# Layer 0's modulation by single row tiles, five summed on TensorE and three as dot products on VectorE, and the first projection in the order of arrival

## The chip, the core and the metric

The kernel runs on one core of a Trainium2 chip. The core has five engines that run at the same time, each through its own list of instructions in a fixed order: TensorE (PE in the profile, with its weight loads as PEld), VectorE (DVE), ScalarE (ACT), GpSimd (POOL) and SyncE (SP), which issues all of this kernel's DMAs. Engines wait for each other through semaphores. The metric is the device time of one execution in microseconds (us); before the change it is 1154.92 us, the median of 3 runs (1154.86 to 1157.67).

## What is computed

Two layers of a transformer-like trunk over 512 latent and 256 context tokens of 1024 channels. Each layer starts with a modulated norm and one combined input projection; two attention branches, gates and an output projection follow. The change touches only what stands ahead of and inside the first projection of layer 0:

```
mod_x = silu(c) @ w_ada + b_ada            # w_ada: 1024 x 3072
shift_x, scale_x, gate_x = split(mod_x, 3)
mod_c = silu(c_ctx) @ w_ada + b_ada
hx = rmsnorm(x, norm_g) * (1 + scale_x) + shift_x
hc = rmsnorm(ctx, norm_g) * (1 + scale_c) + shift_c
px = hx @ w_in ;  pc = hc @ w_in           # first 512 columns: a_k
```

The modulation is a vector times a matrix, for two vectors (c and c_ctx). Its shift and scale parts for layer 0 need 1024 x 2048 numbers of w_ada, 8 MB.

## The kernel before

The 1024 channels are cut into eight slices k of 128, and the 768 tokens into six tiles t of 128. A normed token tile is turned (transposed on PE, L287) into `yT`, where the channels lie on the partitions; so one slice of `hx` needs shift and scale of its 128 channels alone. Every operand of a projection is split into a high and a low part in fp32r, and each product is three matmuls (high by high, high by low, low by high; L341 to L343, the helper `mm3`). The first projection (columns C_AK, 512 of them) keeps six PSUM tiles open, one for each token tile, and adds to each of them slice by slice: 8 slices x 6 tiles x 3 = 144 matmuls.

Its weights come slice by slice (`load_w`): a DMA of 256 KB into one of three `raw` tiles (L309), a cast to `whi` on ACT (L311), and the rest `wlo = raw - whi` on POOL or DVE in turn (L314). A `raw` tile is free for the next load only when its `wlo` is done.

The modulation of layer 0 goes in four parts q of two slices each (`ada_load`, `ada_part`). A part's 2 MB of w_ada come as two DMAs of 1 MB (`rawx`, `rawy`). PE multiplies them by silu(c) and silu(c_ctx), which stand as columns in `scol`, on four column groups of its array side by side (L190); ACT copies the result to a row (L192), PE turns the row (L195), DVE adds the four groups (L197), and `mod_finish` (L171 to L173) makes `modc`, shift and scale. `start_mod` then scales a slice of `yT` on DVE (L298), casts it to the high part of `hx` on ACT (L300) and subtracts for the low part on DVE or POOL (L301). `start_y` (L281 to L289) squares a token tile on ACT, takes the root on POOL, scales on DVE and turns on PE.

The order of the instructions on each engine is set when the program is built, by a scheduler that plays the kernel through with its own costs and times. On the chip each engine keeps to that order: an instruction whose inputs are late holds up all that stand behind it on its engine.

## Time and profile before

| | |
|---|---|
| median of 3 runs | 1154.92 us |
| the profiled execution: its span, first to last instruction | 1153.4 us |
| PE busy | 1123.0 us (97%) |
| DVE busy | 809.8 us (70%) |
| ACT, POOL busy | 573.9 us (50%), 495.0 us (43%) |
| DMA | 134.04 MB, mean 116 GB/s |
| matmuls of the first projection start | 20.70 us |
| first matmul of the next projection (into the next psf tile) | 65.99 us |

Times of the trace are us from the start of the span. A row of the timeline is: start, duration, engine, line, operation, output <- inputs, shapes, how many in a row, and in brackets the idle time before it and what ended it. A duration includes a tail that overlaps the engine's next instruction: matmuls of 0.39 us follow each other every 0.23 us, and VectorE's of 0.69 us every 0.61 us. Rows that are cut out of the list of groups give count, busy time and mean ns of one.

### The profile page before, as it was taken

The page shows a single profiled execution, that of the slowest core. Times are in us where ns is not written, and L with a number is a line of the kernel's source. Part 1 is how long each engine was busy: PE and PEld are TensorE (multiplying, and loading weights), DVE is VectorE, ACT ScalarE, POOL GpSimd, SP SyncE. Part 2 cuts the span into 40 slices and gives each one's busy share as a digit, 9 for nine tenths or more (in the row PEclk, how much of TensorE's full clock was granted, in tenths as well). Part 3 has the DMA queues.
Part 4 walks back from the last instruction along what each step waited for, and adds up shares of the span by engine and source line. Part 5 has one row for each costly group of instructions (what it writes and reads, how often), then busy time and mean ns, then how long its engine had stood idle before and what let it go on. Part 6 is the DMA issues. An engine that isn't in the chain of part 4 may idle for free.

```text
span 1153.4 us, 17280 instructions
## 1 busy us (share of the span) xinstructions
PE 1123.0 (97%) x6078; PEld 949.0 (82%) x6078; DVE 809.8 (70%) x1508; ACT 573.9 (50%) x1167; POOL 495.0 (43%) x459
## 2 busy tenths in 40 slices
PE   5999999999999999999999999999999999999998
PEld 4688888889988888878788787888888988887786
DVE  4566688897464687688587755469787665898563
ACT  5453266666433465566330265346666445766521
POOL 3362354454375243354411126245553664465311
PEclk9999999999999999999999999999999999999999
DMA  9644222233342332470353523543332333142143
GB/s 368 195 126 137 69 85 65 72 115 97 115 130 63 107 102 73 67 276 19 121 172 101 174 74 110 176 106 113 108 105 84 110 101 101 65 173 92 63 129 92
DMA packets 88000, 134.04 MB, mean 116 GB/s; under 512 B 10629, under 2 KB 52585, under 8 KB 86249
## 3 DMA queue, kind: packets, MB, share of 16 engines
q1 hardware_dynamic: 87912, 132.94, 36.8%
q8 instruction: 48, 0.79, 0.3%
q14 instruction: 40, 0.32, 0.1%
HBM read 115.58 MB, written 17.32 MB: 115 GB/s over the span
## 4 chain that ended last, share of the span: by engine, by line
PE 83%; DVE 7%; issue 3%; POOL 2%; ACT 2%; DMA 2%; ACTq 0%; POOLq 0%; DVEq 0%
PE psx L341 12%; PE psx L343 12%; PE psx L342 12%; PE psf L341 9%; PE psf L342 9%; PE psf L343 9%; PE pst L655 5%; PE pss L704 2%; PE pss L705 2%; PE psv L959 2%; PE psv L958 1%; PE pss L781 1%; PE pst L417 1%; DVE wlo L328 1%; DVE ptl L659 1%
## 5 line engine op out<-in xcount | busy, mean ns | idle before, releaser
L659 DVE TENSOR_TENSOR ptl<-pst,pth 128x512 fp32r<-128x512 f32 (+1 forms) x176 | 116.0, 672 | 46.4 <-ACT pth L658 45.4
L658 ACT CAST pth<-pst 128x512 fp32r<-128x512 f32 (+1 forms) x176 | 99.2, 576 | 87.5 <-PE pst L655 56.3
L328 POOL TENSOR_TENSOR wlo<-raw,whi 128x512 fp32r<-128x512 f32 x68 | 95.0, 1402 | 108.9 <-ACT whi L326 87.8
L341 PE MATMUL psf<-hx,whi 128*128 128x512 f32 (+1 forms) x368 | 139.2, 378 | 0.0
L342 PE MATMUL psf<-hx,whi 128*128 128x512 f32 (+1 forms) x368 | 138.1, 375 | 0.0
L343 PE MATMUL psf<-hx,wlo 128*128 128x512 f32 (+1 forms) x368 | 137.8, 374 | 0.0
L341 PE MATMUL psx<-whi,hx 128*128 128x512 f32 (+1 forms) x368 | 137.2, 374 | 0.0
L342 PE MATMUL psx<-wlo,hx 128*128 128x512 f32 (+1 forms) x368 | 135.8, 369 | 0.0
L343 PE MATMUL psx<-whi,hx 128*128 128x512 f32 (+1 forms) x368 | 133.6, 369 | 0.0
L314 POOL TENSOR_TENSOR wlo<-raw,whi 128x512 fp32r<-128x512 f32 x44 | 60.4, 1373 | 140.4 <-ACT whi L311 123.8
L311 ACT CAST whi<-raw 128x512 fp32r<-128x512 f32 x96 | 58.7, 623 | 103.5 <-PE psx L343 38.6
L326 ACT CAST whi<-raw 128x512 fp32r<-128x512 f32 x136 | 82.5, 622 | 50.3 <-DMA raw<-in_w_in_dram 34.1
L655 PE MATMUL pst<-ident,p 128*128 128x128 f32 x640 | 99.9, 272 | 1.4 <-DVE ptl L659 0.9
L328 DVE TENSOR_TENSOR wlo<-raw,whi 128x512 fp32r<-128x512 f32 x68 | 70.2, 1033 | 28.3 <-ACT whi L326 27.8
L655 PEld LDWEIGHTS pst<-ident,p 128*128 128x128 f32 x640 | 77.7, 141 | 13.3 <-DVE ptl L659 1.6
L644 POOL TENSOR_SCALAR r<-r 128x1 f32<-128x1 f32 x64 | 23.1, 361 | 151.7 <-DVE r L639 144.1
L645 POOL TENSOR_TENSOR p<-p,r 128x512 f32<-128x512 f32 (+1 forms) x64 | 83.5, 1304 | 5.0
L341 PEld LDWEIGHTS psx<-whi,hx 128*128 128x128 f32 x368 | 69.6, 189 | 11.8 <-issue 0.8
L343 PEld LDWEIGHTS psf<-hx,wlo 128*128 128x128 f32 x368 | 69.4, 188 | 11.8
L343 PEld LDWEIGHTS psx<-whi,hx 128*128 128x128 f32 x368 | 69.4, 189 | 11.5
L342 PEld LDWEIGHTS psx<-wlo,hx 128*128 128x128 f32 x368 | 69.6, 189 | 11.0
L341 PEld LDWEIGHTS psf<-hx,whi 128*128 128x128 f32 x368 | 69.4, 189 | 10.8 <-ACT zt L502 0.2
(239 smaller groups left out, 3033.4 us busy)
## 6 DMA issues: line engine op xcount, KB each, us to landing
raw<-in_w_in_dram SPq DMA_DIRECT2D x168, 256.0 KB, 2.9
rawb<-in_w_ada_dram SPq DMA_DIRECT2D x64, 256.0 KB, 2.8
gs<-zt SPq DMA_DIRECT2D x32, 256.0 KB, 2.0
raw<-in_w_out_dram SPq DMA_DIRECT2D x32, 256.0 KB, 2.8
tg<-gs SPq DMA_DIRECT2D x4, 1536.0 KB, 7.4
rawx<-in_w_ada_dram SPq DMA_DIRECT2D x4, 1024.0 KB, 7.2
rawy<-in_w_ada_dram SPq DMA_DIRECT2D x4, 1024.0 KB, 12.2
raw<-in_w_o_a_dram SPq DMA_DIRECT2D x16, 256.0 KB, 2.7
```

The lines of the kernel that those rows point to most:

```text
L311: S.copy(hi[:, :n], raw[:, :n])
L314: e.tensor_tensor(lo[:, :n], raw[:, :n], F(hi[:, :n]), ALU.subtract)
L326: S.copy(hi, raw)
L328: lo_eng(i).tensor_tensor(lo, raw, F(hi), ALU.subtract)
L341: T.matmul(ps, lhs[0], rhs[0], start=first, stop=False)
L342: T.matmul(ps, lhs[0], rhs[1], start=False, stop=False)
L343: T.matmul(ps, lhs[1], rhs[0], start=False, stop=last)
L644: G.tensor_scalar(r[:, i:i + 1], r[:, i:i + 1], 0.5, None, ALU.mult)
L645: G.tensor_tensor(p[:, c0:c1], p[:, c0:c1], r[:, i:i + 1].to_broadcast([128, c1 - c0]), ALU.mult)
L655: T.transpose(pt[:, c0:c0 + 128], src, ident)
L658: S.copy(hi[:, n0:n1], pt[:, n0:n1])
L659: V.tensor_tensor(lo[:, n0:n1], pt[:, n0:n1], F(hi[:, n0:n1]), ALU.subtract)
```

## The change

The eight slices of the modulation now go one by one.

- Slices 0 to 4 (`ADA_PE = 5`) go as before over PE, but by single slices: a slice has its own 1 MB of w_ada in two DMAs, 8 matmuls of 256 columns (`ada_sum_pe`), and two transposes, a reduction and `mod_finish` (`ada_turn`). The program's input `w_ada0` is laid out for that and holds five slices.
- Slices 5 to 7 (`ada_wide`, `ada_dots`) take another way: w_ada comes turned, with the channel to be summed along the row, as two tiles of 128x1024 for each slice (one for shift, one for scale), and DVE multiplies each with silu(c) and with silu(c_ctx), spread over all partitions in `cb`, and sums along the row: four dot products of 1024 elements per slice, 12 in all. `cb` is 1 MB, read by two more DMAs.
- The loads, the transposes, the sums and the matmuls of the first projection are written out in one list (`start_run`), and `in_program_order` binds PE and SP to this list. DVE, ACT and POOL are still ordered by the scheduler.
- One more buffer for token tiles (`XB` 6 to 7), which the wide tiles share.

The rest of the program keeps its instructions, and nearly all of its order.

```
--- before.py
+++ after.py
@@ -30,8 +30,9 @@
 GQ_POOL = (1, 3)
 GATES = (3, 3)
 PRE_NA, PRE_GQ = 1, 2
-ON_PE, ON_DVE = mybir.EngineType.PE, mybir.EngineType.DVE
-XB, RX = 6, 2
+ON_PE, ON_DVE, ON_SP = mybir.EngineType.PE, mybir.EngineType.DVE, mybir.EngineType.SP
+XB, RX = 7, 2
+ADA_PE = 5
 
 C_AK, C_AV, C_BKV, C_AQ, C_BQ, C_AZ, C_BZ, C_GA, C_GB = (
     0, 512, 1024, 1280, 1792, 2304, 2816, 3328, 4352)
...
@@ -141,7 +140,6 @@
     csl = stp.tile([16, 128], F32, name="csl")
     V.scalar_tensor_tensor(csl, cth, 1.0, crow, ALU.add, ALU.mult)
     V.tensor_scalar(csl, csl, 0.5, None, ALU.mult)
-    nc.sync.dma_start(cd, csl)
     asum = cp.tile([128, 24, 2, 2], F32, name="asum")
     scol = stp.tile([128, 8, 32], F32, name="scol")
     V.memset(scol, 0.0)
...
@@ -172,31 +170,55 @@
         V.tensor_tensor(sc, sums[:, 1].rearrange("p k v -> p v k"), row(bsc[:, l, k0:k1]), ALU.add)
         V.tensor_tensor(sc, sc, row(g32[:, l, k0:k1]), ALU.mult)
 
-    def ada_load(q, pool):
+    ada_w, ada_pt = {}, {}
+
+    def ada_load(k, pool):
+
+        w = (pool.tile([128, 2048], F32, tag="rawx", name=nm("rawx"), bufs=RX) if k < RX
+             else big("rawy")[:, 0:2048]).rearrange("p (k n) -> p k n", k=8)
+        for h in range(2):
+            nc.sync.dma_start(w[:, 4 * h:4 * h + 4], w_ada0[k, :, 4 * h:4 * h + 4, :])
+        ada_w[k] = w
+
+    def ada_sum_pe(k, pool):
+
+        pt = psw(256, "t")
+        w = ada_w.pop(k)
+        for h in range(2):
+            for j in range(4):
+                T.matmul(pt[32 * j:32 * j + 32], scol[:, 4 * h + j, :], w[:, 4 * h + j, :], start=h == 0, stop=h == 1)
+        row = pool.tile([128, 256], F32, tag="row", name=nm("row"), bufs=1)
+        S.copy(row, pt)
+        ada_pt[k] = row
+
+    def ada_turn(k, pool):
+
+        row = ada_pt.pop(k)
+        pt = psw(256, "t")
+        for f in range(2):
+            T.transpose(pt[:, 128 * f:128 * f + 128], row[:, 128 * f:128 * f + 128], ident)
+        sums = pool.tile([128, 2, 1, 2], F32, tag="sums", name=nm("sums"))
+        V.tensor_reduce(sums.rearrange("p a k v -> p (a k) v"),
+                        pt.rearrange("p (f j v) -> p f v j", f=2, j=4)[:, :, 0:2, :], AX, ALU.add)
+        mod_finish(0, sums, k, k + 1)
+
+    def ada_wide(k, pool):
 
         ws = []
-        for h in range(2):
-            w = (pool.tile([128, 2048], F32, tag="rawx", name=nm("rawx"), bufs=RX) if h == 0
-                 else big("rawy")[:, 0:2048]).rearrange("p (k n) -> p k n", k=4)
-            nc.sync.dma_start(w, w_ada0[q, :, 4 * h:4 * h + 4, :])
+        for a in range(2):
+            w = pool.tile([128, DM], F32, tag="x", name=nm("wx"), bufs=XB)
+            nc.sync.dma_start(w.rearrange("p (h n) -> p h n", h=2), w_ada[0, :, 8 * a + k].rearrange("h p n -> p h n"))
             ws.append(w)
-        return ws
-
-    def ada_part(q, ws, pool):
-
-        pt = psw(512, "t")
-        for h, w in enumerate(ws):
-            for j in range(4):
-                T.matmul(pt[32 * j:32 * j + 32], scol[:, 4 * h + j, :], w[:, j, :], start=h == 0, stop=h == 1)
-        row = pool.tile([128, 512], F32, tag="row", name=nm("row"), bufs=1)
-        S.copy(row, pt)
-        pt = psw(512, "t")
-        for f in range(4):
-            T.transpose(pt[:, 128 * f:128 * f + 128], row[:, 128 * f:128 * f + 128], ident)
-        sums = pool.tile([128, 2, 2, 2], F32, tag="sums", name=nm("sums"))
-        V.tensor_reduce(sums.rearrange("p a f v -> p (a f) v"),
-                        pt.rearrange("p (f j v) -> p f v j", f=4, j=4)[:, :, 0:2, :], AX, ALU.add)
-        mod_finish(0, sums, 2 * q, 2 * q + 2)
+        ada_w[k] = ws
+
+    def ada_dots(k, cb, pool):
+
+        sums = pool.tile([128, 2, 1, 2], F32, tag="sums", name=nm("sums"))
+        for a, w in enumerate(ada_w.pop(k)):
+            for v in range(2):
+                o = w if v else pool.tile([128, DM], BF16, tag="jk", name=nm("jk"), bufs=1)
+                V.tensor_tensor_reduce(o, w, cb[:, v, :], 1.0, 0.0, ALU.mult, ALU.add, sums[:, a, 0, v:v + 1])
+        mod_finish(0, sums, k, k + 1)
 
     def ada_steps(l, tiles, halves, nv, pool):
 
...
@@ -384,6 +400,16 @@
                 tc.add_manual_dep(i, last, mybir.DependencyInfo(
                     mybir.DependencyClass.NoSync, mybir.DependencyReason.DATA), reason="program order")
                 last = i.name
+
+    def in_program_order(engines, n):
+
+        last = {}
+        for i in nc.cur_bb.bb.instructions[n:]:
+            if i.engine in engines:
+                if i.engine in last:
+                    tc.add_manual_dep(i, last[i.engine], mybir.DependencyInfo(
+                        mybir.DependencyClass.NoSync, mybir.DependencyReason.DATA), reason="program order")
+                last[i.engine] = i.name
 
     def turn_late(n):
 
...
@@ -581,14 +607,8 @@
         kav = big("ka").rearrange("p (j n) -> p j n", j=4)
         if first:
             w, pss = [], [psw() for t in range(6)]
-            for q in range(4):
-                if q == 0:
-                    mid(0, lambda: w.extend(load_w(W, C_AK, 512, 2, mix_lo)))
-                if q < 3:
-                    mid(q + 1, lambda: w.extend(load_w(W, C_AK, 512, 2, mix_lo, 2 * q + 2)))
-                start_mods(q)
-                for t in range(6):
-                    tok_mm(pss[t], w, 512, a_hx, t, 2 * q, 2 * q + 2)
+            mid(lambda k: w.extend(load_w(W, C_AK, 512, 1, mix_lo, k)),
+                lambda t, k: tok_mm(pss[t], w, 512, a_hx, t, k, k + 1))
             es_n.close()
             st_es.close()
             hp["p"] = bgp_es.enter_context(tc.tile_pool(name=f"cp{l}", bufs=1, reuse_waits="tile"))
...
@@ -1039,26 +1059,99 @@
                 run(late, len(late))
 
 
-    ada_w = {}
-
-    def start_part(q, load):
-
-        if q == 0:
-            ada_w[0] = ada_load(0, npool)
-            load()
-            for t in range(2, 6):
-                load_x(t)
-            ada_w[1] = ada_load(1, npool)
-            for t in range(2):
-                start_y(t, npool, yT)
-        else:
-            load()
-            if q < 3:
-                ada_w[q + 1] = ada_load(q + 1, npool)
-        ada_part(q, ada_w.pop(q), npool)
-        if q == 0:
-            for t in range(2, 6):
-                start_y(t, npool, yT)
+    def start_run(load_k, mm):
+
+        on_pe = lambda fn, *a: fn(*a)
+        n0 = len(nc.cur_bb.bb.instructions)
+
+        def ys(*ts):
+            for t in ts:
+                on_pe(start_y, t, npool, yT)
+
+        def mods(k, *cuts):
+            start_mod(k, yT, hx0, *cuts)
+
+        def mms(ts, ks):
+            for k in ks:
+                for t in ts:
+                    on_pe(mm, t, k)
+
+        add = lambda k: on_pe(ada_sum_pe, k, npool)
+        trn = lambda k: on_pe(ada_turn, k, npool)
+        load_x(0)
+        ada_load(0, npool)
+        load_x(1)
+        load_k(0)
+        ada_load(1, npool)
+        load_k(1)
+        nc.sync.dma_start(cd, csl)
+        load_x(2)
+        load_x(3)
+        ys(0)
+        add(0)
+        trn(0)
+        mods(0, 0, 128)
+        ys(1)
+        mms((0,), (0,))
+        add(1)
+        mods(0, 128, 256)
+        ada_load(2, npool)
+        load_k(2)
+        mms((1,), (0,))
+        trn(1)
+        mods(1, 0, 256)
+        load_x(4)
+        load_x(5)
+        ys(2)
+        mms((0, 1), (1,))
+        ys(3)
+        mods(0, 256, 512)
+        mods(1, 256, 512)
+        ada_load(3, npool)
+        load_k(3)
+        cb = npool.tile([128, 2048], F32, tag="rawx", name=nm("cbw"), bufs=RX).rearrange("p (v n) -> p v n", v=2)
+        for v in range(2):
+            nc.sync.dma_start(cb[:, v, :], cd[8 * v:8 * v + 8].rearrange("k p -> (k p)").unsqueeze(0)
+                              .to_broadcast([128, DM]))
+        add(2)
+        mms((2, 3), (0,))
+        trn(2)
+        mods(2, 0, 512)
+        mms((2, 3), (1,))
+        ys(4)
+        mms((0, 1), (2,))
+        ys(5)
+        ada_load(4, npool)
+        load_k(4)
+        mms((2, 3), (2,))
+        add(3)
+        for k in range(3):
+            mods(k, 512, 768)
+        mms((4, 5), (0,))
+        trn(3)
+        mods(3, 0, 768)
+        ada_wide(5, npool)
+        load_k(5)
+        mms((4, 5), (1, 2))
+        add(4)
+        mms((0, 1, 2), (3,))
+        trn(4)
+        mods(4, 0, 768)
+        ada_wide(6, npool)
+        load_k(6)
+        mms((3, 4, 5), (3,))
+        ada_dots(5, cb, npool)
+        mods(5, 0, 768)
+        ada_wide(7, npool)
+        load_k(7)
+        mms(range(6), (4,))
+        ada_dots(6, cb, npool)
+        mods(6, 0, 768)
+        mms(range(6), (5,))
+        ada_dots(7, cb, npool)
+        mods(7, 0, 768)
+        mms(range(6), (6, 7))
+        in_program_order((ON_PE, ON_SP), n0)
 
     hx1 = []
 
...
@@ -1082,8 +1175,8 @@
     rpb = d.pop('rpb')
     d['cvec'] = np.concatenate([d['c'].reshape(8, 128), d['c_ctx'].reshape(8, 128)])
     d['x'] = d['x'].reshape(1, ROWS, GRID_W, DM).transpose(0, 2, 1, 3).reshape(1, NLAT, DM)
-    a0 = d['w_ada'][0].reshape(8, 128, 3, 4, 256)[:, :, :2]
-    d['w_ada0'] = a0.transpose(3, 1, 0, 2, 4).reshape(4, 128, 8, 512)
+    a0 = d['w_ada'][0].reshape(8, 128, 3, 8, 128)[:, :, :2, :ADA_PE]
+    d['w_ada0'] = a0.transpose(3, 1, 0, 2, 4).reshape(ADA_PE, 128, 8, 256)
 
     d['w_ada'] = d['w_ada'].reshape(2, 2, 512, 24, 128).transpose(0, 1, 3, 4, 2)
     norms = [np.concatenate([d[n][l], d[n][l]])[None] for l in range(2) for n in ('q_norm_a', 'k_norm_a')]
```

Where the order moved: first, VectorE at the last modulations that come over PE. Before, this is the last of the four parts, slices 6 and 7 (`yT_104` holds slices 4 to 7, `hx_100` and `hx_102` their high and low parts):

```order
L314 TENSOR_TENSOR wlo_725<-raw_721,whi_723 128x512
L314 TENSOR_TENSOR wlo_737<-raw_733,whi_735 128x512
L197 TENSOR_REDUCE sums_513<-pst_508 128x8
L171 TENSOR_TENSOR modc<-sums_513,gcol 128x2x2
L172 TENSOR_TENSOR modc<-sums_513,bsc 128x2x2
L173 TENSOR_TENSOR modc<-modc,g_132 128x2x2
L298 TENSOR_SCALAR yT_104<-yT_104,modc 128x512
L298 TENSOR_SCALAR yT_104<-yT_104,modc 128x256
L298 TENSOR_SCALAR yT_104<-yT_104,modc 128x512
L298 TENSOR_SCALAR yT_104<-yT_104,modc 128x256
```

After, this is slice 4, the last that comes over PE (`sums_514`); `sums_542` is slice 5, `wx_469` and `wx_471` are its two wide tiles, `raw_560` is the weight slice 7 and `raw_781` the second weight slice of the next projection:

```order
L201 TENSOR_REDUCE sums_514<-pst_511 128x4
L220 ISA jk_543,sums_542<-wx_469,cbw_333 128x1024
L220 ISA sums_542 128x1
L169 TENSOR_TENSOR modc<-sums_514,gcol 128x2
L170 TENSOR_TENSOR modc<-sums_514,bsc 128x2
L336 TENSOR_TENSOR wlo_564<-raw_560,whi_562 128x512
L220 ISA wx_469,sums_542<-wx_469,cbw_333 128x1024
L220 ISA sums_542 128x1
L220 ISA jk_546,sums_542<-wx_471,cbw_333 128x1024
L220 ISA sums_542 128x1
L171 TENSOR_TENSOR modc<-modc,g_127 128x2
L336 TENSOR_TENSOR wlo_785<-raw_781,whi_783 128x512
```

The first dot products and two splits of weights have come between the reduction for slice 4 and the last step of its modulation (`L171`). The scaling of slice 4 by it follows only after two more dot products:

```order
L169 TENSOR_TENSOR modc<-sums_542,gcol 128x2
L220 ISA wx_471,sums_542<-wx_471,cbw_333 128x1024
L220 ISA sums_542 128x1
L220 ISA jk_585,sums_584<-wx_523,cbw_333 128x1024
L220 ISA sums_584 128x1
L320 TENSOR_SCALAR yT_104<-yT_104,modc 128x512
L320 TENSOR_SCALAR yT_104<-yT_104,modc 128x256
```

Second, TensorE at the same place of the first projection. After, the turn of slice 4 (`row_500`) stands in the middle of the matmuls of slice 3 (`whi_329`), and the matmuls of slice 4 (`whi_421`) follow at once:

```order
L199 MATMUL pst_511<-ident,row_500 128x128 x2
L363 MATMUL psx_136<-whi_329,hx_99 128x512
L364 MATMUL psx_136<-wlo_331,hx_99 128x512
L365 MATMUL psx_136<-whi_329,hx_101 128x512
L363 MATMUL psx_137<-whi_329,hx_99 128x512
L364 MATMUL psx_137<-wlo_331,hx_99 128x512
L365 MATMUL psx_137<-whi_329,hx_101 128x512
L363 MATMUL psx_138<-whi_329,hx_99 128x512
L364 MATMUL psx_138<-wlo_331,hx_99 128x512
L365 MATMUL psx_138<-whi_329,hx_101 128x512
L363 MATMUL psf_133<-whi_421,hx_100 128x512
L364 MATMUL psf_133<-wlo_423,hx_100 128x512
```

Before, the turn of the last part (`row_506`, slices 6 and 7) stood inside the matmuls of slices 4 and 5 (`whi_406`, `whi_412`), with 14 of these behind it and ahead of slice 6:

```order
L342 MATMUL psx_141<-wlo_408,hx_100 128x512
L343 MATMUL psx_141<-whi_406,hx_102 128x512
L341 MATMUL psx_141<-whi_412,hx_100 128x512
L195 MATMUL pst_508<-ident,row_506 128x128 x4
L342 MATMUL psx_141<-wlo_414,hx_100 128x512
L343 MATMUL psx_141<-whi_412,hx_102 128x512
L341 MATMUL psx_142<-whi_406,hx_100 128x512
L342 MATMUL psx_142<-wlo_408,hx_100 128x512
```

Third, ScalarE at the same place: after, the casts of `hx` for slices 4 and 5 (`hx_100`, in the last row but one of this piece) stand behind the casts of the weights of slice 7 (`raw_560`) and of four weight slices of the next projection.

```order
L322 CAST hx_99<-yT_103 128x768
L333 CAST whi_529<-raw_527 128x512
L191 COPY row_500<-pst_491 128x256
L333 CAST whi_562<-raw_560 128x512
L333 CAST whi_777<-raw_775 128x512
L333 CAST whi_783<-raw_781 128x512
L333 CAST whi_789<-raw_787 128x512
L333 CAST whi_795<-raw_793 128x512
L322 CAST hx_100<-yT_104 128x768 x2
L333 CAST whi_801<-raw_799 128x512
```

11 lines of the change are left out of this document (2 added, 9 removed).

## The prediction

> **What bounds the kernel now.** I read the page first, its busy shares and the chain that ended last:
>
> ```profile
> span 1153.4 us, 17280 instructions
> PE 1123.0 (97%) x6078; PEld 949.0 (82%) x6078; DVE 809.8 (70%) x1508; ACT 573.9 (50%) x1167; POOL 495.0 (43%) x459
> PE 83%; DVE 7%; issue 3%; POOL 2%; ACT 2%; DMA 2%; ACTq 0%; POOLq 0%; DVEq 0%
> ```
>
> TensorE is the bound; it is idle for 1153.4 - 1123.0 = 30.4 us. VectorE's 70% is an average, so I asked for busy times by stretch: from the first transposes to the point from which PE never stops, from there to the end of the first projection, and the stage behind it (columns: stretch, its length, then busy time and count of PE, PEld, DVE, ACT and POOL, the granted clock, the DMA share, GB/s):
>
> ```profile
> 8.97:38.26 29.29, 24.22 (x141) 16.32 (x141) 16.29 (x37) 14.56 (x29) 8.91 (x12) 0.94 0.98 391
> 38.26:65.30 27.04, 27.04 (x129) 20.93 (x130) 13.94 (x26) 11.81 (x20) 11.96 (x8) 1.00 0.45 128
> 65.30:140.00 74.70, 74.70 (x349) 61.62 (x348) 50.39 (x105) 26.42 (x46) 33.86 (x32) 1.00 0.39 113
> ```
>
> PE waits only in the first stretch, with DMA at 98%; from 38.26 on it is full, in the first projection and behind it. Outside the first 65 us the change moves hardly any instruction. So the change is worth what it moves the end of the first projection, and that shift goes through to the end of the kernel. The timeline of PE gives that end, 65.99, where the next projection takes the psf tile:
>
> ```profile
> 8.97 3.62 PE L287 MATMUL pst<-ident,x 128*128 128x128 f32 x16 [3.90 <-DVE x L283]
> 38.26 0.50 PE L341 MATMUL psf<-whi,hx 128*128 128x512 f32 x1 [0.67 <-ACT hx L300]
> 65.77 0.39 PE L343 MATMUL psx<-whi,hx 128*128 128x512 f32 x1
> 65.99 0.39 PE L341 MATMUL psf<-whi,hx 128*128 128x512 f32 x1
> ```
>
> **TensorE's work, before and after.** The chain of waits lists PE by start to start:
>
> ```profile
> 21.05 0.43 PE psf L341
> 29.35 0.44 PE pst L287 x4
> 30.50 1.85 PE pst L190 x16
> 35.30 0.45 PE pst L195 x4
> 60.94 1.13 PE psx L343 x5
> ```
>
> A projection matmul is 1.13/5 = 0.226 us (0.43 while the array is slow after a wait), a transpose 0.44/4 = 0.11, the sum of a part 1.85, its turn 0.45. Before: 144 matmuls 32.5, 48 transposes 5.3, four sums 7.4, four turns 1.8: 47.0 us. After: the same 32.5 and 5.3, five sums of half the columns 5 x 0.93 = 4.6, ten transposes 1.1: 43.5 us. A matmul of 256 columns is not in the trace; between no gain from halving (five sums at 1.85, PE 4.6 us worse) and half, I take half: the row's 1.85 us are for two slices, and the new sum is one of them. So the change takes 3.5 us off PE. That is all it can give where PE is full.
>
> **The price is on VectorE.** The three wide slices cost it 12 dot products of 1024. The same instruction with 512 elements stands in the trace, and a two-input operation in two widths (timeline of DVE):
>
> ```profile
> 92.03 0.68 DVE L220 CUSTOM_DVE_ANT_0 junk<-rawb,cb 128x512 bf16<-128x512 f32 x1
> 92.64 0.08 DVE L220 DVE_READ_ACCUMULATOR2_ANT asum<- 128x1 f32 x1
> 92.76 0.69 DVE L220 CUSTOM_DVE_ANT_0 rawb<-rawb,cb 128x512 f32<-128x512 f32 x1
> 93.37 0.69 DVE L220 CUSTOM_DVE_ANT_0 junk<-rawb,cb 128x512 bf16<-128x512 f32 x1
> 54.80 0.19 DVE L197 TENSOR_REDUCE sums<-pst 128x8 f32<-128x32 f32 x1 [2.21 <-PE pst L195]
> 55.50 1.65 DVE L298 TENSOR_SCALAR yT<-yT,modc 128x512 f32<-128x512 f32 x4
> 57.27 0.96 DVE L301 TENSOR_TENSOR hx<-yT,hx 128x768 fp32r<-128x768 f32 x1
> 60.13 0.68 DVE L314 TENSOR_TENSOR wlo<-raw,whi 128x512 fp32r<-128x512 f32 x1
> ```
>
> Two dots of 512 take 93.37 - 92.03 = 1.34, so 0.67 each; 256 more columns cost 0.96 - 0.68 = 0.28, so a dot of 1024 is 0.67 + 0.56 = 1.23. Bounds: 0.67 if width cost nothing, 1.34 if it were two of 512. Twelve take 14.8 us.
>
> Where they lie decides. In the new order of DVE all twelve stand behind the reduction for slice 4 (`sums_514`), which waits for a turn that PE has in the middle of slice 3. DVE keeps its order, so it can't begin them when their tiles land. Between that reduction and the last low part of `hx` (slice 7) I count: 12 dots 14.8; three splits of weights at 0.61, 1.8; four scalings of a slice at 1.65/2, less the tail, 0.79, 3.2; three low parts at 0.9, 2.7; 13 small steps at 0.12 (six steps of 54.80 to 55.50 are 0.70), 1.6. Sum 24.1 us of one engine, with nothing beside it that could be swapped in.
>
> POOL adds to it. When POOL splits weights, a DVE operation beside it is late:
>
> ```profile
> 40.87 1.77 DVE L314 TENSOR_TENSOR wlo<-raw,whi 128x512 fp32r<-128x512 f32 x1
> ```
>
> ```profile
> 40.54 1.55 POOL L314 TENSOR_TENSOR wlo<-raw,whi 128x512 fp32r<-128x512 f32 x1 [0.41 <-ACT whi L311]
> 38.28 1.85 POOL L301 TENSOR_TENSOR hx<-yT,hx 128x768 fp32r<-128x768 f32 x1 [2.87 <-ACT hx L300]
> ```
>
> 1.77 in place of 0.68, to 0.55 us behind POOL's end at 42.09. On average over the first 66 us the groups of DVE say how much:
>
> ```profile
> L314 DVE TENSOR_TENSOR wlo<-raw,whi 128x512 fp32r<-128x512 f32 x7 | 6.0, 851 | 10.4 <-ACT whi L311 10.4
> L301 DVE TENSOR_TENSOR hx<-yT,hx 128x768 fp32r<-128x768 f32 x4 | 4.8, 1206 | 2.0 <-ACT hx L300 1.9
> L300 ACT CAST hx<-yT 128x768 fp32r<-128x768 f32 x6 | 5.0, 834 | 10.5 <-DVE yT L298 10.5
> ```
>
> (851 - 680) x 7 + (1206 - 960) x 4 = 2.2 us over 11 operations, 0.2 each; the stretch has 18 such (12 dots, 3 splits, 3 low parts): 3.6 us. Ends: 0, and about 7 if each of POOL's three splits and its 768-wide low part holds DVE for its whole time (3 x 1.55 + 1.85 = 6.5). I take 3.6.
>
> [...]
>
> **When that stretch of DVE begins.** PE's list up to the turn of slice 4: 48 transposes 5.3, five sums 4.6, 8 + 2 transposes 1.1, and 63 matmuls (slices 0 to 2, and three tiles of slice 3) 14.2: 25.2 us. PE starts at 8.97 as before, since the first token tile is the fourth load in both orders. Before, the stretch 8.97 to 38.26 held 48 transposes, three sums, two turns and 36 matmuls, 5.3 + 5.6 + 0.9 + 8.1 = 19.9 us, and took 29.3; 9.4 were lost to waits and to the slow array. The new front has shorter waits for loads, but five chains through ACT and DVE (sum, copy, turn, reduce, scale, cast) where two lay there. I take the same 9.4; ends 3 (one slow start) and 13. So the turn ends at 8.97 + 25.2 + 9.4 = 43.6, and slice 3 two us later.
>
> **The sum.** DVE ends its stretch at 43.6 + 24.1 + 3.6 + 0.3 (the last wait for a cast) = 71.6. Slice 6 needs the same list less slice 7's low part, so its low part is there at 70.7, and its first two matmuls are done by then; what is left of slices 6 and 7 is 34 x 0.226 = 7.7 us. PE ends the first projection at 78.4, in place of 65.99: 12.4 us later. On the way PE stands for some 9 us: the scaling of slice 4 lies behind seven dots' and splits' worth of DVE, 5 x 1.23 + 2 x 0.61 + 0.9 + 0.8 + 1.4 for POOL = 10.5 us behind the turn, and the cast (0.83) follows. Slice 5 waits in the same way and is done before slice 6. So the wait for loads is replaced by a longer one for DVE. Span 1153.4 + 12.4 = 1165.8; the median of the runs lies 1.5 above the profiled span, so **1167 us**.
>
> What else the change adds costs nothing there. `cb` (1 MB) and the loads run while PE is behind. ACT's casts of later weights stand ahead of `hx` of slice 4; the last of them needs a `raw` tile that DVE's split of weight slice 7 frees at about 47, and by the page's list of DMA issues a load takes 2.9 us:
>
> ```profile
> raw<-in_w_in_dram SPq DMA_DIRECT2D x168, 256.0 KB, 2.9
> ```
>
> Two loads in a row and a cast end by 52, and the scaling comes at 54; were they later than that, every us would count.
>
> **The rivals.**
> 1. **PE stays full, faster.** If DVE's dots were hidden, PE's 43.5 us and the old loss of 9.4 end at 61.9: 4.1 us earlier, 1151. For it: DVE is busy for only 13.94 of 27.04 us in the second stretch. Against it: that spare time, 13.1, is less than the 14.8 of the dots, and the order puts them all into the last third. Chance 0.08.
> 2. **No change.** Were nothing lost at the front but 3 us, the turn would end at 37.2; with no POOL collisions DVE would end at 61.6, PE at 68.4; with dots at 1.0 us in place of 1.23, at 65.6. Needs three ends at once. Chance 0.07.
> 3. **Slower still, by the loads.** DVE's list has the split of weight slice 7 (`raw_560`) right behind its first dot, and it is the 35th load, 14.8 MB in. The windows of a full DMA and of one that reads rows of 2 KB (columns as above):
>
> ```profile
> 5.00:30.00 25.00, 16.70 (x92) 12.78 (x92) 13.96 (x33) 13.63 (x27) 8.86 (x14) 0.93 1.02 422
> 100.00:110.00 10.00, 10.00 (x46) 8.19 (x45) 8.80 (x18) 3.98 (x7) 3.61 (x3) 1.00 0.77 236
> ```
>
> The first token tile is read at 5.9 with 0.6 MB in. At 422 GB/s the rest lands 33.6 us later, at 39.5; the 5.2 MB of 2 KB rows at 236/0.77 = 306 add 4.7, 44.2. DVE is there at 45: just in time. But SP waits for `raw` tiles already now,
>
> ```profile
> SPq L309 <- POOL wlo L314: 18.0, 7, 4.7
> ```
>
> and one such wait of 4.7 us would put the load to 49 and all behind it with it: 4 us more, and with POOL's upper end 3 more, 1174. Chance 0.2. The point from which it decides: a landing behind 45.
> My forecast, slower by DVE's list, has 0.65.
>
> **How the numbers follow.** 0.3% is 3.5 us, about what a measurement tells from no change. Faster 0.08 (rival 1, just over it), same 0.07, slower 0.85. The range: the low end has the turn at 39 and half of POOL's price, 12.4 - 4.6 - 1.8 = 6 us, 1161, and I go on to 1158 towards rival 2; the high end is rival 3 at 1174.
>
> **What would show it.** In the changed trace: DVE without a gap of note from the reduction for slice 4 on, 23 to 30 us long, with 12 dots of about 1.2; a wait of PE of 8 to 11 us before slice 4, put down to `hx` on ACT and behind it to `yT` on DVE; the next projection's psf tile at 76 to 81. Behind that, PE full as before. Wrong would be dots that run before the turn of slice 4 or take under 0.9 us, or PE at 95% or more from 30 to 65.

## The result: 1171.03 us, and the profile after

| | before | after |
|---|---|---|
| median, same chip | 1154.89 us (1154.51 to 1157.67) | 1171.03 us (1169.60 to 1171.63) |
| ratio, 95% interval | | 1.0132 (1.0118 to 1.0146): slower |
| span of the profiled execution | 1153.4 us | 1169.8 us |
| first projection ends (next one takes psf) | 65.99 us | 80.44 us |
| from there to the end of the span | 1087.4 us | 1089.4 us |

Of 16.4 us in the span, 14.45 lie in the stretch that the prediction is about and 2.0 behind it. The page of the changed kernel (span; busy times; shares of the chain that ended last):

```profile
span 1169.8 us, 17363 instructions
PE 1126.5 (96%) x6088; PEld 949.2 (81%) x6088; DVE 829.3 (71%) x1547; ACT 574.6 (49%) x1170; POOL 496.8 (42%) x460
PE 79%; DVE 10%; issue 4%; POOL 2%; ACT 2%; DMA 2%; SPq 0%; POOLq 0%; DVEq 0%; ACTq 0%
```

The shares hardly tell it. Busy times by stretch do (columns as in the prediction: PE, PEld, DVE, ACT, POOL, clock, DMA share, GB/s):

```profile
9.00:46.00 37.00, 31.60 (x197) 20.99 (x197) 20.26 (x49) 19.41 (x40) 12.53 (x17) 1.00 0.90 352
46.00:82.00 36.00, 24.38 (x93) 18.41 (x92) 30.24 (x57) 11.10 (x18) 10.86 (x8) 0.86 0.34 99
82.00:157.00 75.00, 75.00 (x353) 61.84 (x352) 50.22 (x101) 24.15 (x43) 34.68 (x30) 1.00 0.36 108
```

Before, PE was full from 38.26 on. Now it is idle for 11.6 us of the middle stretch, where VectorE has 30.24 of 36, and full again behind it. The waits of TensorE from 46 to 82 name whom it waits for (line waited at, engine and tile waited for: us in total, times, longest):

```profile
PE psf L363 <- ACT hx L322: 9.4, 2, 8.2
PE psf L365 <- DVE hx L323: 2.3, 2, 1.8
```

And the timeline of TensorE: first the front, then the turn of slice 4, the first matmul of slice 4 and its first with the low part, two later waits, and the next projection.

```profile
8.79 1.94 PE L309 MATMUL pst<-ident,x 128*128 128x128 f32 x8 [4.24 <-DVE x L305]
10.66 1.94 PE L189 MATMUL pst<-rawx,scol 128*32 128x256 f32 x16
...
18.45 1.85 PE L189 MATMUL pst<-rawx,scol 128*32 128x256 f32 x16
...
27.58 1.07 PE L189 MATMUL pst<-rawy,scol 128*32 128x256 f32 x16 [0.35 <-DVE yT L311]
...
46.49 0.38 PE L199 MATMUL pst<-ident,row 128*128 128x128 f32 x2
...
57.17 0.79 PE L363 MATMUL psf<-whi,hx 128*128 128x512 f32 x1 [8.24 <-ACT hx L322]
...
60.21 0.79 PE L365 MATMUL psf<-whi,hx 128*128 128x512 f32 x1 [1.82 <-DVE hx L323]
...
71.38 0.50 PE L363 MATMUL psf<-whi,hx 128*128 128x512 f32 x1 [1.12 <-ACT hx L322]
...
80.44 0.39 PE L363 MATMUL psf<-whi,hx 128*128 128x512 f32 x1
```

What VectorE does meanwhile, in its timeline: the reduction for slice 4, a dot product, three operations that took longer than their like, the scaling of slice 4, and the last low parts.

```profile
46.91 0.17 DVE L201 TENSOR_REDUCE sums<-pst 128x4 f32<-128x16 f32 x1 [2.86 <-PE pst L199]
...
49.01 1.21 DVE L220 CUSTOM_DVE_ANT_0 wx<-wx,cbw 128x1024 f32<-128x1024 f32 x1
...
53.19 2.27 DVE L220 CUSTOM_DVE_ANT_0 jk<-wx,cbw 128x1024 bf16<-128x1024 f32 x1
...
55.39 0.86 DVE L320 TENSOR_SCALAR yT<-yT,modc 128x512 f32<-128x512 f32 x2
...
64.44 2.86 DVE L220 CUSTOM_DVE_ANT_0 jk<-wx,cbw 128x1024 bf16<-128x1024 f32 x1
...
67.22 1.24 DVE L171 TENSOR_TENSOR modc<-modc,g 128x2 f32<-128x2 f32 x1
...
71.55 1.94 DVE L323 TENSOR_TENSOR hx<-yT,hx 128x768 fp32r<-128x768 f32 x2
```

From 46.91 to 73.49 VectorE has 26.5 us of work in 26.6. The three long rows (53.19, 64.44 and 67.22) each lie beside one of these on POOL:

```profile
52.60 1.78 POOL L336 TENSOR_TENSOR wlo<-raw,whi 128x512 fp32r<-128x512 f32 x1 [5.35 <-ACT whi L333]
64.24 1.97 POOL L323 TENSOR_TENSOR hx<-yT,hx 128x768 fp32r<-128x768 f32 x1 [9.87 <-ACT hx L322]
66.90 1.55 POOL L336 TENSOR_TENSOR wlo<-raw,whi 128x512 fp32r<-128x512 f32 x1 [0.70 <-ACT whi L333]
```

### The profile page after: what moved, and what is told of

It reads as the page before. It is cut to its first block, busy times and chain, and to the rows that moved or that the text cites. A ratio compares the mean times of both kernels' runs of the same rounds, so it can differ in the third digit from the quotient of the medians.

```text
span 1169.8 us, 17363 instructions
## 1 busy us (share of the span) xinstructions
PE 1126.5 (96%) x6088; PEld 949.2 (81%) x6088; DVE 829.3 (71%) x1547; ACT 574.6 (49%) x1170; POOL 496.8 (42%) x460
## 4 chain that ended last, share of the span: by engine, by line
PE 79%; DVE 10%; issue 4%; POOL 2%; ACT 2%; DMA 2%; SPq 0%; POOLq 0%; DVEq 0%; ACTq 0%
PE psx L363 11%; PE psx L365 11%; PE psx L364 11%; PE psf L363 9%; PE psf L365 9%; PE psf L364 9%; PE pst L675 4%; PE pss L724 2%; PE pss L725 2%; PE psv L979 2%; PE pss L801 1%; PE psv L978 1%; PE pst L443 1%; DVE ptl L679 1%; DVE wlo L350 1%
## 5 line engine op out<-in xcount | busy, mean ns | idle before, releaser
L363 PE MATMUL psf<-hx,whi 128*128 128x512 f32 (+1 forms) x368 | 139.3, 378 | 0.0
L363 PE MATMUL psx<-whi,hx 128*128 128x512 f32 (+1 forms) x368 | 138.2, 377 | 0.5 <-ACT hx L322 0.5
L365 PE MATMUL psx<-whi,hx 128*128 128x512 f32 (+1 forms) x368 | 136.2, 370 | 0.0
L350 DVE TENSOR_TENSOR wlo<-raw,whi 128x512 fp32r<-128x512 f32 x68 | 70.0, 1031 | 27.6 <-ACT whi L348 26.6
L363 PEld LDWEIGHTS psx<-whi,hx 128*128 128x128 f32 x368 | 70.1, 190 | 13.0 <-ACT hx L322 1.4
L363 PEld LDWEIGHTS psf<-hx,whi 128*128 128x128 f32 x368 | 69.4, 189 | 10.8 <-ACT zt L528 0.3
```

What stands on the lines that cost most here:

```text
L350: lo_eng(i).tensor_tensor(lo, raw, F(hi), ALU.subtract)
L363: T.matmul(ps, lhs[0], rhs[0], start=first, stop=False)
L365: T.matmul(ps, lhs[1], rhs[0], start=False, stop=last)
```

## The experiments

Each run's "turn" is the start of the two transposes for slice 4, its "end" the first matmul of the next projection. Six kernels whose TensorE lists are the same up to there differ by 2.0 us at the turn (45.34 to 47.35), one profiled execution each, so the third column is the better one for what follows it.

| kernel | turn | end | turn to end | ratio to before, 95% |
|---|---|---|---|---|
| the change | 46.49 | 80.44 | 33.95 | 1.0132 (1.0118 to 1.0146) |
| six dots | 45.52 | 77.09 | 31.57 | 1.0116 (1.0096 to 1.0136) |
| no dots | 45.34 | 66.10 | 20.76 | 1.0020 (1.0009 to 1.0031) |
| scaling of slice 4 first | 47.35 | 82.19 | 34.84 | 1.0146 (1.0126 to 1.0166) |
| six dots, scalings first | 45.42 | 72.35 | 26.93 | 1.0078 (1.0058 to 1.0098) |
| order not bound | 44.42 | 78.73 | 34.31 | 1.0127 (1.0107 to 1.0147) |
| all on TensorE, turn just ahead | 46.77 | 77.15 | 30.38 | 1.0092 (1.0075 to 1.0109) |
| all on TensorE, longer lead | 44.99 | 69.98 | 24.99 | 1.0034 (1.0022 to 1.0046) |

The letters of theories below are each explained in the text that uses them. A is always the prediction's: the list of dot products on VectorE behind the turn of slice 4 sets the end.

**Half the dot products.** In `ada_dots`:

```
-            for v in range(2):
-                o = w if v else pool.tile([128, DM], BF16, tag="jk", ...)
+            V.memset(sums[:, a, 0, 1:2], 0.0)
+            for v in range(1):
+                o = w if not v else pool.tile([128, DM], BF16, tag="jk", ...)
```

> Leaves out the dot products for the context's vector (six of the 12); the sums for it are set to zero, so the modulation of slices 5 to 7 for context tokens is the bias alone. All loads stay. Theory A (the length of VectorE's list behind the turn of slice 4 sets the end): six dots at 1.22 us are 7.3 us less, the first projection ends at 73 in place of 80.4, the kernel at about 1163. Theory B (not the length, but that the scaling of slice 4 stands far down in that list, so that PE gets slice 4 late and then has 16 us of its own work left): only the dots ahead of that scaling count, three of five, 3.7 us, so about 1167; less still if something else in the list takes their place. Theory C (loads): 1170.

1168.51 us: only 2.5 less than with all twelve, by two runs of 1166.81 and 1170.22; in the trace the end comes 3.35 us sooner. That is nearer to theory B (3.7 or less) than to the 7.3 us of theory A. Why so little is in two places of its profile, the waits of TensorE from 45 on and the last low parts on VectorE:

```profile
PE psf L364 <- ACT hx L323: 7.2, 1, 7.2
PE psf L366 <- DVE hx L324: 2.8, 1, 2.8
```

```profile
62.47 1.94 DVE L324 TENSOR_TENSOR hx<-yT,hx 128x768 fp32r<-128x768 f32 x2
```

VectorE is done at 64.4, 12.7 us before the end, so its length decides no longer. What decides is that the scaling of slice 4 still stands behind four dots and two splits; TensorE starts slice 4 only 2.0 us sooner than with twelve dots (55.14), waits once more, for its low part (59.12), and then never again: it is its own 70 matmuls, the first of them slow behind the wait (0.79 and then 0.63 us, from 63.45 on 0.40), that end at 77.

**All eight slices on TensorE.** Slices 5 to 7 go like 0 to 4. Between a slice's turn and its own first matmul stand the next slice's sum and nine matmuls, 3.0 us; for slice 7, the last, only nine matmuls.

```
-ADA_PE = 5
+ADA_PE = 8
...
+        add(5)
         mms((3, 4, 5), (3,))
-        ada_dots(5, cb, npool)
+        mms((0, 1, 2), (4,))
+        trn(5)
         mods(5, 0, 768)
```

> All eight slices summed on TensorE, in the same list and with TensorE and SyncE bound to it; no dots, no wide tiles, no spread vector (1 MB less to load). Theory A (the dots): nothing is left that holds VectorE, TensorE has 47 us of work as before and loses 9.4 at the front, ends at 65 to 67; 1154 to 1157. Theory D (the list by single slices, with twice as many chains of sum, copy, turn, reduction, scaling and cast, loses time by itself): the first projection ends at 72 to 76, 1162 to 1166.

1165.95 us, ratio 1.0092: without a single dot product most of the loss was still there. At this point I held the short lead of the new list to be the main cause of the change's loss, and the dots for a small part of it. The next runs show that this was the wrong inference: the run takes away one stall and puts another in its place.

**The scaling of slice 4 ahead of the dots of slice 5.** VectorE's instructions of `ada_dots(5)` are bound behind the scaling:

```
+        n1 = len(nc.cur_bb.bb.instructions)
         ada_dots(5, cb, npool)
+        after(scaled[4], n1)
```

> The change with one more rule for VectorE: the dots of slice 5 come behind the scaling of slice 4. No instruction is added or taken. Theory A: the wait of 8 us that TensorE has ahead of slice 4 goes away and comes back ahead of slice 5, VectorE's list is as long as before, the first projection ends at 80 to 81 as in the change, 1170 to 1172. Theory B: slice 4 comes 8 us earlier and the end with it, about 1163.

1171.96 us, no gain. TensorE's waits for the high parts of `hx`, over the whole execution:

```profile
PE psf L366 <- ACT hx L325: 14.1, 4, 10.5
```

Slice 4 waits only 0.5 us for its high part and 1.0 for its low part, slice 5 waits 10.5 us: the wait has moved one slice on. With twelve dots it is the length of the list, not the place in it.

**TensorE and SP not bound to the written list.** 

```
-        in_program_order((ON_PE, ON_SP), n0)
```

> The change without the binding of TensorE and SyncE to the list: the scheduler orders all engines. The dots stay. Theory A: the dots lie in VectorE's list all the same, 1168 to 1173. Theory D (the list costs): near 1160.

1169.76 us. From the turn to the end it takes 34.31 us, as the change does. The scheduler spreads the waits (from 45 on `PE psf L363 <- ACT hx L322` is 8.1 us in four waits of at most 3.5). With the 0.8 for a low part they are 8.9 us in place of 11.6, but the end stays as far behind the turn, and VectorE is as full: it is busy for 26.93 of the 27 us from 45 to 72. The binding isn't the cause.

**No dot products at all.**

```
-            for v in range(2):
-                o = w if v else pool.tile([128, DM], BF16, tag="jk", ...)
-                V.tensor_tensor_reduce(o, w, cb[:, v, :], 1.0, 0.0, ...)
+            V.tensor_copy(sums[:, a, 0, :], w[:, 0:2])
```

> All 12 dot products are left out: for slices 5 to 7 the two columns of sums are copied from the first two columns of each wide tile, so the modulation of these slices is not computed; the loads, the list of TensorE and the scalings stay. The first projection ended at 80.44 with 12 dots and at 77.09 with six. Theory A (dots set it, each as much as the others): another 3.4 us, end at 73.7, some 1164 us. Theory F (what is behind the turn of slice 4 is one list on VectorE; once it is shorter than TensorE's own list, TensorE sets the end): turn at 46.9, then 81 matmuls at 0.226 are 18.3 us, and 2 to 4 us for the chain from the turn to slice 4: end at 67 to 69, that is 1157 to 1159 us. Neither gives a gain over the kernel before, since the front has lost 3 us more than before.

1157.54 us, ratio 1.0020. TensorE at the turn, at slice 4, at its first low part and at the end:

```profile
45.34 0.38 PE L199 MATMUL pst<-ident,row 128*128 128x128 f32 x2
...
48.44 0.50 PE L361 MATMUL psf<-whi,hx 128*128 128x512 f32 x1 [0.67 <-ACT hx L320]
...
50.11 0.50 PE L363 MATMUL psf<-whi,hx 128*128 128x512 f32 x1 [0.93 <-DVE hx L321]
...
66.10 0.39 PE L361 MATMUL psf<-whi,hx 128*128 128x512 f32 x1
```

The waits of 8.24 and 1.82 have become 0.67 and 0.93. From the turn to the end the twelve dots cost 33.95 - 20.76 = 13.2 us, by the two ratios (1.0132 - 1.0020) x 1155 = 12.9. So nearly all of the loss is theirs. In this order the first six cost 10.8 of it and the last six 2.4, for the reason given at the run with six. Even with the dots free, though, the list doesn't beat the kernel before.

**A longer lead on TensorE.** Again all eight slices on TensorE, but the sum and the turn of slices 5 to 7 are issued about a slice of matmuls sooner:

```
-        mms((0, 1, 2), (3,))
+        mms((0, 1), (3,))
         trn(4)
...
+        mms((2, 3), (3,))
+        add(5)
+        mms((4, 5), (3,))
+        trn(5)
...
+        mms((0, 1, 2), (4,))
+        add(6)
+        mms((3,), (4,))
+        trn(6)
+        mms((4, 5), (4,))
+        add(7)
+        mms((0,), (5,))
+        trn(7)
...
```

> All eight slices are summed on TensorE, as in the earlier run that did so and ended the first projection at 77.15 (1166 us), but the sum and the turn of slices 5 to 7 are issued about one slice of matmuls (4 us) sooner, so that the chain turn, reduction, scaling, cast, low part (3.5 to 4 us) lies behind matmuls of the slice before. Theory D' (the short lead is what cost that run 8.3 us between 45 and 75): the loss there falls to 1 or 2 us, end at 69 to 71, 1157 to 1160 us. Rival G (single slices cost by themselves, by the slow array and by VectorE's small steps, wherever they lie): end stays at 75 to 77, 1164 to 1166 us.

1159.38 us, ratio 1.0034, end at 69.98. The waits of TensorE from 45 on, first with the turn just ahead, then with the longer lead:

```profile
PE psf L363 <- ACT hx L322: 3.2, 2, 1.8
PE psf L365 <- DVE hx L323: 0.8, 2, 0.5
PE psf L365 <- POOL hx L323: 0.7, 1, 0.7
```

```profile
PE pst L199 <- ACT row L191: 1.1, 1, 1.1
```

So the stall of the earlier run was its own. Its waits are 4.6 us in all, and its trace puts them down to more than one cause. The chain of slice 4, from the turn over the reduction, the scaling and the cast to the low part, took 3.8 us (46.77 to 50.60) and was just in time. Slice 5 waited 0.7 us for its low part, which POOL ended at 57.12. Slice 6 waited 2.3 us: VectorE had scaled it by 60.86, but on ScalarE its cast stood behind casts of weights that waited for their loads (the scaling on VectorE, then ScalarE):

```profile
59.99 0.87 DVE L320 TENSOR_SCALAR yT<-yT,modc 128x512 f32<-128x512 f32 x2
```

```profile
60.40 0.62 ACT L333 CAST whi<-raw 128x512 fp32r<-128x512 f32 x1 [3.62 <-DMA raw<-in_w_in_dram]
62.16 0.62 ACT L333 CAST whi<-raw 128x512 fp32r<-128x512 f32 x1 [1.14 <-DMA raw<-in_w_in_dram]
...
63.46 0.83 ACT L322 CAST hx<-yT 128x768 fp32r<-128x768 f32 x1
```

Slice 7 waited 1.6 us, with only nine matmuls, about 2 us, behind its turn. Now two sums and 18 matmuls, over 6 us, stand between the turn of slice 5 and its first matmul, and of these waits none is left, only one of 1.1 us for the row of a turn; how much of that is due to each cause wasn't separated. Now the three slices have three prices, against the run without dots: as dots 33.95 - 20.76 = 13.2 us; on TensorE with the turn just ahead 30.38 - 20.76 = 9.6; on TensorE with the longer lead 24.99 - 0.68 - 20.76 = 3.6 (the turn stands three matmuls, 0.68 us, further ahead there). The last is TensorE's own work for them, 3 x (1.0 + 2 x 0.11) = 3.7.

**A longer lead for slices 3 and 4 too.** The sums and turns of slices 3 and 4 go ahead of matmuls that stood before them, so that more work lies behind these turns; the turns of slices 5 to 7 move too. Against the run before:

```
-        mms((2, 3), (1,))
         ys(4)
-        mms((0, 1), (2,))
-        ys(5)
+        mms((2, 3), (1,))
...
-        mms((2, 3), (2,))
         add(3)
+        ys(5)
+        trn(3)
...
-        mms((4, 5), (0,))
-        trn(3)
         mods(3, 0, 768)
+        mms((0, 1), (2,))
...
-        mms((4, 5), (1, 2))
+        mms((2, 3), (2,))
         add(4)
-        mms((0, 1), (3,))
+        mms((4, 5), (0,))
         trn(4)
...
+        mms((4, 5), (1, 2))
...
```

> As the run with the longer lead, and all six token tiles and the matmuls of tiles 4 and 5 are also put behind more matmuls of tiles 2 and 3, so that there is more work behind the turns of slices 3 and 4 too. Theory D': another 1 us at most from the waits between 45 and 75, end at 68 to 70; what is left over the kernel before (65.99) is the front's loss of 3 us, and 1157 to 1159 us. Rival G: 75 to 77, 1164 to 1166 us.

1161.08 us, ratio 1.0050 (1.0033 to 1.0068); the end is at 71.17, outside of both figures. From 45 to 72 TensorE is full:

```profile
45.00:72.00 27.00, 27.00 (x155) 20.20 (x154) 13.36 (x30) 11.60 (x21) 8.91 (x7) 1.00 0.44 128
```

So theory D' held for the place it speaks of, and the end is 1.2 us later all the same. Ahead of 45 TensorE isn't idle for longer than in the run before (5.2 us in place of 5.4 from its first transposes on), but it works more slowly: the transposes of the third and fourth token tile took 1.47 and 1.78 us in place of 1.09 and 1.04. This profile is of the slowest of four runs (1158.73 to 1163.10), and the intervals of the two ratios overlap, so a cost of the order itself isn't shown. No wait is left to take away behind 45; what remains against the kernel before is ahead of it.

**Half the dots, each slice's behind the scaling of the slice before.** The `ada_dots` of the first run, and the binding of the third for three slices:

```
         ada_dots(5, cb, npool)
+        after(scaled[4], n1)
...
         ada_dots(6, cb, npool)
+        after(scaled[5], n1)
...
         ada_dots(7, cb, npool)
+        after(scaled[6], n1)
```

> The six dot products for the context vector are left out (its sums are set to zero), as in the earlier run that ended at 77.09; and the dot products of each wide slice are forced behind the scaling of the slice before. Theory A (the length of VectorE's list sets the end, the place of the dots in it does not): 76 to 78, as without the forced order, and the waits of TensorE move from slice 4 to slice 5 and 6. Theory P (with half the dots there is room, and the early scaling lets TensorE work while VectorE sums): end at 73 to 75, some 1164 us.

1164.19 us, end at 72.35: theory P, and a little better. With twelve dots the place didn't matter, with six it is worth 31.57 - 26.93 = 4.6 us. Theory A in its plain form, that only the length counts, holds only while VectorE's list is the longer one.

**TensorE kept busy in the front.** The sums of slices 0 and 1 start to start take 1.8 to 1.9 us, the later ones 1.0. `warm` issues transposes of the identity that nobody reads:

```
+        def warm(n):
+            pt = psw(256, "t")
+            for i in range(n):
+                T.transpose(pt[:, 0:128], ident, ident)
...
+        warm(18)
         ys(0)
```

> The changed kernel, with 18 transposes of the identity on TensorE ahead of the first token tile's, where it waits 4.24 us; nobody reads what they write. In the changed kernel the first eight transposes take 1.94 us and the sums of slices 0 and 1 take 1.86 and 1.78, where the later sums take 1.00: an array that has just stood works at half speed. Theory H (this slowness is part of the 3 us that the front lost): the first eight transposes take about 0.9 and the first sum 1.0, the turn of slice 4 comes 1 to 2 us sooner than 46.5, and the first projection ends at 78.5 to 79.5, some 1169 us. Rival L (the front waits for loads and for chains through other engines, and what TensorE saves it waits): the same durations fall, but the turn stays at 46.2 or later and the end at 80 or later, 1170 to 1171 us.

> The list with all eight slices on TensorE and the longer lead, whose first projection ended at 69.98 (1159.4 us), with such transposes at four places: 18 ahead of the first token tile, 4 behind the sum of slice 0, 10 behind the second and 10 behind the third token tile, where TensorE waited 4.3, 0.5, 1.4 and 1.7 us. Theory H: no sum takes over 1.1 any more, end at 67 to 69, 1156 to 1158 us. Rival L: 69.5 to 71 (the added transposes themselves cost up to 1 us where they are longer than the wait), 1159 us or more.

> The kernel before, with 18 transposes of the identity ahead of the first token tile's 16, and 12 more behind the turn of the first part, where TensorE waits 2.9 us. Before, those 16 take 3.62 us where 16 later ones take 1.8 to 2.0. Theory H: they take 1.8, and the first projection ends at 64 to 65 in place of 65.99, 1153 to 1154 us, a gain of 0.1 to 0.2%. Rival L: the second token tile and w_ada's first part land no sooner, so the end stays within 0.3 of 65.99 and the time at 1154.5 to 1156.

The changed kernel with `warm`: TensorE's first transposes and first sum, a turn, the second token tile's transposes behind a wait, then the turn of slice 4:

```profile
8.58 1.09 PE L309 MATMUL pst<-ident,x 128*128 128x128 f32 x8 [0.80 <-DVE x L305]
10.02 1.07 PE L189 MATMUL pst<-rawx,scol 128*32 128x256 f32 x16 [0.35 <-DVE yT L311]
12.18 0.44 PE L199 MATMUL pst<-ident,row 128*128 128x128 f32 x2 [1.08 <-ACT row L191]
14.25 1.94 PE L309 MATMUL pst<-ident,x 128*128 128x128 f32 x8 [1.64 <-DVE sums L201]
...
44.56 0.38 PE L199 MATMUL pst<-ident,row 128*128 128x128 f32 x2
```

The durations fell as both theories said (1.94 to 1.09, 1.94 to 1.07), until, behind two waits of 1.08 and 1.64, the array was slow again at 14.25 (1.94 us for the eight transposes, and 0.63 and 0.61 for the second and third matmul behind them, in place of 0.40 at 18.72 and 18.96). The turn is at 44.56, at least 0.8 us ahead of every other run with this front, and the end at 79.12, 1.3 us ahead of the change's; the time, 1171.08 us with the same ratio of 1.0132 (1.0116 to 1.0147), shows no gain, and such an interval can't show 1.3 us. This run leaves it open. With the longer lead the same addition at four places ended at 70.81 in place of 69.98, 1162.22 us, ratio 1.0054 (1.0040 to 1.0067): rival L. From its first transposes to 45 TensorE is idle for 4.9 us in place of 5.4 and busy for 31.4 in place of 30.7, the added transposes included. The intervals of the two ratios overlap, so no gain is shown, and no loss either.

In the kernel before it did gain: 1153.55 us, ratio 0.9982 (0.9973 to 0.9990), the end at 63.36 in place of 65.99. Its TensorE:

```profile
8.53 1.10 PE L287 MATMUL pst<-ident,x 128*128 128x128 f32 x8 [0.15 <-DVE x L283]
10.36 1.17 PE L287 MATMUL pst<-ident,x 128*128 128x128 f32 x8 [0.73 <-ACT yT L289]
...
17.10 0.50 PE L341 MATMUL psf<-whi,hx 128*128 128x512 f32 x1 [0.74 <-ACT hx L300]
```

The end comes sooner than theory H gave, and there is a second difference: the scheduler had moved the third token tile's transposes behind the first six matmuls. So one more run has that order without the added transposes (a binding of the third tile's transposes behind the matmuls of slice 0 by tiles 0 and 1):

```
+                    start_mods(0, (0, 256))
+                    for t in range(2):
+                        tok_mm(pss[t], w, 512, a_hx, t, 0, 1)
+                    mid(None, range(2, 6))      # start_y of tiles 2 to 5, bound behind the matmuls above
```

> The kernel before, without any added transposes, but with the transposes of the third token tile bound behind the first six matmuls of the first projection, as they stood in the run of the kernel before with transposes of the identity (there the scheduler had moved them by itself). That run ended the first projection at 63.36 in place of 65.99, 1153.55 us. Theory O (the order did it: before, the first matmul waited behind a token tile that was not there): first matmul at 18 to 19, end at 63.5 to 64.5, 1153.5 to 1154.5 us. Theory H (the array's speed did it): the first 16 transposes take 3.6 us again and the end is at 65.3 to 66.3, no gain.

```profile
8.80 4.01 PE L287 MATMUL pst<-ident,x 128*128 128x128 f32 x16 [4.51 <-DVE x L283]
...
18.62 0.50 PE L341 MATMUL psf<-whi,hx 128*128 128x512 f32 x1 [2.43 <-ACT hx L300]
...
65.67 0.39 PE L341 MATMUL psf<-whi,hx 128*128 128x512 f32 x1
```

1155.36 us, ratio 1.0000 (0.9991 to 1.0009), as theory H has it. The order alone gives nothing; together with the added transposes, behind which the first 16 of the token tiles took 2.3 us in place of 3.6, the gain is 0.18%. That kernel, the one before with 30 transposes that nobody reads, is the fastest of this study. Whether the transposes alone, in the order of before, would give as much wasn't tried.

## Why the prediction was right, and where its sum was off

The direction, the mechanism and the time were right: 1167 forecast, 1171.03 measured, within the range. Point by point:

- **What bounds.** Right. The shift at the end of the first projection, 14.45 us, is 88% of the span's 16.4.
- **The list on VectorE.** Right: no gap, all twelve dots behind the turn, 26.6 us long (28.0 forecast, 23 to 30 named as its sign). The base was a little too dear: 26.6 - 3.8 = 22.8 in place of 24.1 + 0.3. Start to start, as the prediction counts, a dot takes 1.14 to 1.15 us (50.15 to 51.30), not 1.23: 1.0 us over twelve. The 13 small steps take 1.2, not 1.6, mostly 0.07 to 0.08 each; the 0.12 was misread besides, for the rows from 54.80 to 55.50 are four steps, not six. And the last wait for a cast, 0.3, didn't come.
- **POOL.** 3.6 forecast; the three long rows have 2.27 - 1.21, 2.86 - 1.21 and 1.24 - 0.15, together 3.8. The size was right, its distribution not, and that the total fits is luck: not 0.2 for each of 18 operations, but two dots and a small step that were held. The trace shows where each of them ends: 53.19 + 2.27 = 55.46 is POOL's end of 54.38 plus 1.08; 64.44 + 2.86 = 67.30 is 66.21 plus 1.09; the small step ends at 68.46, as POOL does at 68.45. The upper end of 6.5 wasn't reached: it has four operations of POOL hold VectorE for their whole time, and here three did, each for about what it had left, 1.19, 1.77 and 1.23 us (a fourth, the end of the split at 45.97, cost the first dot 0.08).
- **The wait ahead of slice 4.** 8.24 us against some 9, put to `hx` on ACT and behind it on VectorE, as named.
- **The step that was mis-sized: when that stretch begins.** The prediction took the front's loss as before's, 9.4 us, and so the end of the turn at 43.6. It was at 46.87: 46.87 - 8.79 - 25.2 = 12.9 us lost. The two windows say in what: TensorE was idle for 37.0 - 31.6 = 5.4 us, hardly more than before's 29.29 - 24.22 = 5.1. The rest is work that took longer than priced. Five sums were put at 5 x 0.93 = 4.6; less a tail of 0.07 they took 1.87 + 1.78 + 3 x 1.0 = 6.65, the first two while the array was slow. What the other 1.2 us went into isn't worked out here. The end of 13 named for this unknown was the right one. It also differs from run to run: other kernels with this TensorE list turned slice 4 between 45.34 and 47.35, all of them behind the 43.4 that the sum would give for the same row.
- **The sum.** 46.9 + 26.6 + 6.95 = 80.44 in place of 43.6 + 28.0 + 6.8 = 78.4: the front 3.3 too small, VectorE 1.4 too large. The two errors partly cancel, which is luck.
- **"Behind that, PE full as before."** Nearly. From the end of the first projection to the end of the span the change takes 2.0 us longer than before: TensorE is idle for 18.1 us there in place of 17.0, and busy for 0.9 longer with the same 5805 instructions. Over all kernels of the study this part lies between 1087.4 and 1090.1 us, with no pattern that I can tie to the edits; the cause stays open, and it is half of the error of the forecast.
- **The rivals.** Rival 3, the loads, didn't come: VectorE split weight slice 7 at 48.41 without a wait, its cast having been done by 45.9; and the last of the weight casts ahead of `hx` of slice 4 ended at 53.15, 3.1 us before the scaling was done. Rivals 1 and 2 needed hidden dots or no loss at the front; neither was there.
- **What the prediction hadn't seen.** It priced the dots against a TensorE that would otherwise be full, and that holds for the list as it was (no dots: 0.67 and 0.93 us of waits). But it would have let a reader think that putting the three slices back on TensorE recovers the loss; with the same short lead it recovers 1169.8 - 1165.0 = 4.8 us of the span's 16.4.

## What to carry to other kernels

Before work is moved to an engine with spare time, look at when that time is: here VectorE was idle for 13 us of the stretch in the kernel before, but all twelve dot products stood in its order behind a wait for TensorE, and so became a chain of 26.6 us. A producer that feeds the full engine slice by slice needs a lead as long as its whole chain (3.8 us for slice 4 with the turn just ahead), together with what stands ahead of that chain in the order of each engine; and an experiment that takes one stall away is to be read beside one that takes away the other too, or the wrong one gets the blame.

## What the runs showed of the hardware

- The same 16 matmul instructions of a sum took 1.94 us (10.66), 1.85 (18.45) and 1.07 (27.58 and later), and 16 transposes 3.6 to 4.0 us or 2.3 (8.53 and 10.36 in the kernel before with `warm`). The granted clock (the third number from the end) shows one slow stretch and not the other: behind the wait of 8.24 us it is 0.50, in the change's slow start 1.00.

```profile
57.17:64.20 7.03, 5.21 (x11) 3.63 (x12) 7.03 (x15) 0.83 (x1) 0.00 (x0) 0.50 0.13 37
8.79:12.60 3.81, 3.81 (x24) 2.13 (x24) 0.69 (x1) 2.14 (x4) 0.81 (x2) 1.00 0.92 355
```

  In the changed kernel with `warm`, 18 transposes in 3.54 us (from 4.24 on) ahead brought the next eight from 1.94 to 1.09. Not every wait is followed by slow work: in the change, behind one of 1.73 us (24.06), the first matmul took 0.50 us and the next 0.40. How long a wait must be to bring a slow stretch the runs don't tell.
- A VectorE operation on two columns, 0.15 us by itself, took 1.24 us beside POOL (67.22). In the three rows here (53.19, 64.44 and 67.22) POOL's operation had 1.19, 1.77 and 1.23 us left, and the meeting cost 1.06 and 1.65 us for two dots of 1.21 and 1.09 for this small step.
